# Weight block rows 528 bytes apart, and two tiles of one projection in 256-column products

## The chip, the cores and the metric

The kernel runs on one core of a Trainium2 chip. The metric is the device time of one execution in microseconds (us), smaller is better; the program has one launch. A core has five engines that work side by side and wait for each other through semaphores: TensorE multiplies matrices (its matrix work is "PE" in the profile, the loading of the stationary operand is "PEld"), VectorE is "DVE", ScalarE is "ACT", GpSimd is "POOL", and SyncE, "SP", mostly issues DMA transfers between HBM and the on-chip memory SBUF. TensorE reads both operands from SBUF and writes its sums into PSUM.

One matmul instruction of this kernel has a *stationary* operand (128 partitions by 128 columns, loaded first) and a *moving* operand (128 partitions by up to 512 columns, streamed past it). Both are rows of 4-byte numbers in each of the 128 partitions; where such a row begins within a partition is its address.

## The reference

The reference is one encoder block for 1024 tokens of width 1024 in float32, with d_ff = 2816:

```python
h = layer_norm(x, ln_in_g, ln_in_b)
proj = h @ w_in[l]                                  # 1024 x 11776, one combined projection
att = dilated_attention(aq, ak, av, slopes)         # 512 wide
rec = hgrn2(hq, hf_fwd, hf_bwd, hi, hg, ...)        # 1024 wide, chunkwise recurrence
merged = sigmoid(ga) * (att @ w_att_up[l]) + sigmoid(gh) * (rec @ w_hgrn_up[l])
h = layer_norm(ALPHA * h + merged @ w_o[l], ...)
gate, up = split(h @ w_ffn_in[l], 2, axis=-1)
h = layer_norm(ALPHA * h + (silu(gate) * up) @ w_ffn_out[l], ...)
```

## The kernel before

**Products.** Every large matrix product is done with numbers split in two: `hi` is the value rounded to the type float32r, `lo` is the rest. `mm3` (lines 270 to 274) issues three matmuls for one block: hi with hi (line 272), the stationary hi with the moving lo (line 273), the stationary lo with the moving hi (line 274). Such a matmul of 128x128 by 128x512 is called a *product* here; there are 7596 of them. `split` (line 211 on) makes the pair: ScalarE casts (line 214), then GpSimd or VectorE subtracts (line 224).

**Granules.** `granules` (line 253) hands out a pair of tiles `w_hi` and `w_lo` of 128 x 4 x 128 numbers from the pool `wp`: four weight blocks side by side, 2048 bytes a partition, with four buffers of each, so eight tiles. A block is 512 bytes of a partition. `weights`, `prep` in `stream`, `product` in `wino_project`, `next_weights` and the row tiles of the W_o stage all take their stationary blocks from there. In `ffn_out` the inner function `weights` (line 1889 on) takes the same tiles flat, as one 512-column moving operand, and the stationary blocks come from the pool `ws`.

**Where tiles lie.** Pools are stacked from two sides of SBUF: `wp` is the first from the right, and all other pools of the right side lie below it; constants are the first from the left. Two pads, `CST_PAD` of 32 bytes and `SMT_PAD` of 704 bytes, shift the left side. In the compiled program the stationary and the moving operand of each of the 7596 products begin 480 bytes past a multiple of 512. The difference of the two addresses modulo 512 bytes is called the *place* here; before the change it is 0 in every product.

**Stages.** Phase 0 and 1 (up to about 1162 us): the input layer norm and the combined projection, done by `stream` with a seven-product form of block matrix multiplication for each 2 x 2 group of blocks; between its groups the attention and recurrence units issue small float32 matmuls and transposes. Phase 2: `att @ W_a` (192 products, 1168.3 to 1211.8 us), in eight tiles `d`, each two halves of 512 tokens by four blocks by three products through `project_many` (line 279); then `rec @ W_r` and the product with W_o. Phase 3: `ffn_in` with the seven-product form, 84 products a step (7 by 4 blocks by 3), and `ffn_out`.

**Order.** A planner with a cost model orders the instructions of each engine when the program is built. Some orders are written by hand (`behind`, `ordered`, `queued`), and evacuations of PSUM run at high priority. Weights are split three products ahead (`prep(i + 3)`).

Of the kernel before, what the change touches and what calls it, by code (L numbers as in the profile page):

```python
# [11 lines left out]
F32R = mybir.dt.float32r  # L12
# [10 lines left out]
HALF = 512  # L23
# [56 lines left out]
class Block:  # L80
# [169 lines left out]
    def queued(self, dst, src):  # L250
        self.ordered("loads", self.nc.sync.dma_start(dst, src))

    def granules(self, pool=None, bufs=4):

        p = pool or self.wp
        return [p.tile([128, 4, 128], F32R, name=n, tag=n, bufs=bufs) for n in ("w_hi", "w_lo")]

    def weights(self, w, r0, nk, c0, pool=None, bufs=2, tag="wraw"):

# [7 lines left out]
            out += [(hi[:, k, :], lo[:, k, :]) for k in range(4)]  # L267
        return out

    def mm3(self, ps, whi, wlo, xhi, xlo, first, last, **kw):  # L270
        nc = self.nc
        nc.tensor.matmul(ps, whi, xhi, start=first, stop=False, **kw)  # L272
        nc.tensor.matmul(ps, whi, xlo, start=False, stop=False, **kw)  # L273
        self.product = nc.tensor.matmul(ps, wlo, xhi, start=False, stop=last, **kw).ins.name  # L274
# [1114 lines left out]
    def phase2(self):  # L1389
        nc = self.nc  # L1390
        with ExitStack() as es:
# [14 lines left out]
            def mrow(k, h):  # L1406
                return m1[:, k, :] if h else m0[k // 2][:, k % 2, :]
            sp = self.sp

            def tgate(i):  # L1410
                t = sp.tile([128, T], F32, name="tg", tag="gate", bufs=2)
                nc.sync.dma_start(t, self.tg_d[i])
                return t

            def up(d):
                return self.weights(self.wa, 0, 4, 128 * d, bufs=1, tag=f"wraw{d % 2}")

            wa = [up(0), up(1)]
            for d in range(8):
                t = tgate(d)  # L1420

                def evac(h, ps, d=d, t=t):
                    s = slice(HALF * h, HALF * (h + 1))
                    nc.vector.scalar_tensor_tensor(mrow(d, h), t[:, s], 1.0, ps, op0=OP.add, op1=OP.mult)

                self.load_split(sp, self.rec_d[d], self.rh[:, d, :], self.rl[:, d, :])
                self.project_many([(self.wa, 4, 128 * d, evac, wa.pop(0))], self.ah, self.al)
                if d < 6:
                    wa.append(up(d + 2))
            wo = [[mp.tile([128, KT, HALF], F32R, name=f"wo0{n}") for n in ("hi", "lo")]]  # L1430
# [17 lines left out]
            for d in range(8):  # L1448
                t = tgate(8 + d)
# [8 lines left out]
                c = d // 2 + 4 * (d % 2)  # L1458
# [11 lines left out]
            for z in (rows, self.recp, self.stp):  # L1470
# [4 lines left out]
                       for n in ("t1", "b11", "b21", "t2")}  # L1475
            yp = es.enter_context(self.pool("yp"))
            w11 = [(yp if k < 3 else self.ws).tile([128, HALF], F32, name="w11", tag=f"w11{k}" if k < 3 else "wsum",
                                                   bufs=1 if k < 3 else 3) for k in range(4)]
# [330 lines left out]
    def ffn_out(self):  # L1809
# [4 lines left out]
        nc, NP = self.nc, NF // 2  # L1814
        with ExitStack() as es:
# [25 lines left out]
            loaded, raws, ready, last, t2s = 0, {}, {}, {}, {}  # L1841
# [32 lines left out]
                return hi, lo  # L1874

            def weights(src):
                hi, lo = (z.rearrange("p k c -> p (k c)") for z in self.granules())
                self.split(hi, lo, src, eng_lo="dve", key="sums")
                return hi, lo

# [12 lines left out]
            def prep(i):  # L1893
                nonlocal loaded
                if i >= len(seq):
                    return
                p, f = seq[i]
                a = acts(p, f)
                while i and loaded < min(len(loads), 4 + 3 * i // 2):
                    load(*loads[loaded])  # L1900
                    loaded += 1
                src = t2s[f] if p == 6 else W[{1: "11", 2: "21", 5: "11", 7: "12", 3: "22"}[p], f]
                ready[i] = a, weights(src)
                for z in todo.get(i, ()):
                    extra(*z)
# [44 lines left out]
            for i, (p, f) in enumerate(seq):  # L1950
# [3 lines left out]
                if p in (1, 6) and 4 <= f < 8:  # L1954
                    t = f if p == 6 else f - 4
                    self.queued(Y[t], self.ahs_d[t])
                if p == 5 and f < 2:
                    t, v = (g2, b2)[f], self.ln["2"][f]
                    self.queued(t, bass.AP(tensor=v.tensor, offset=v.offset, ap=[[0, 128], [1, D]]))
                for g in range(4):  # L1960
                    if f == 0 and p == 2:
                        banks[g][1] = self.ps_sd()
                    c = slice(128 * g, 128 * (g + 1))
# [25 lines left out]
            for c, (g, f0) in enumerate(chunks):  # L1989
# [4 lines left out]
                for k in range(min(4, NP - f0)):  # L1994
                    z = slice(128 * k, 128 * (k + 1))
                    self.mm3(banks[g][0], ahi[:, z], alo[:, z], *last[f0 + k], False, f0 + k == NP - 1,
                             skip_group_check=True)
# [45 lines left out]
```

## Time and profile before

| what | value |
|---|---|
| time, three runs | 2034.79, 2037.7 and 2040.7 us; median 2037.7 us |
| profiled execution | span of 2034.2 us from the first to the last instruction; no other time of it is given |
| granted TensorE clock, mean | 0.998 of full speed |
| products of 512 columns | 7596, about 0.227 us from one start to the next |
| matmuls in all, as recorded | 11002 |
| HBM traffic | 200.77 MB read, 94.11 MB written |

The span leaves out what lies around the program's first and last instruction; beside the median of the runs it is 3.5 us shorter. In the group rows a matmul's own duration includes its way through the array and overlaps the next one, so the pace is read from starts: a product that shows 389 ns begins about 227 ns after the one before it. Float32 matmuls (the small ones) are recorded as two passes.

### The profile page before, as it was taken

The numbers are of one execution on the slowest core, as the hardware profiler recorded it, in microseconds if no ns is written. First come the engines' busy times: TensorE is split into PE (matmuls) and PEld (weight loads), VectorE is DVE, ScalarE is ACT, GpSimd is POOL, SyncE is SP. The second block draws the span as 40 slices with busy tenths as digits, with TensorE's granted clock in tenths as the row PEclk, the third lists the DMA queues.
The fourth block names the chain that finished last, engine by engine and source line by source line (L and its number), as shares of the span: only waits on it lengthen the run. The fifth ranks groups of instructions, "written<-read, shape, count | busy, mean of one in ns | idle before, by whom it ended". The sixth has DMA issues, their size and how long they took to land. (4 is left out here: it accounts for less than half of the span.)

```text
span 2034.2 us, 31011 instructions
## 1 busy us (share of the span) xinstructions
PE 2005.5 (99%) x11002; PEld 1666.0 (82%) x11002; DVE 1310.3 (64%) x2065; ACT 961.4 (47%) x1980; POOL 1026.6 (50%) x890
## 2 busy tenths in 40 slices
PE   7999999999999999999999999999999999999998
PEld 5788888788888888888888888888788888888886
DVE  7777545884458843778444226557776776767788
ACT  6654455554655535665465433244433333344541
POOL 6656644676446663466545662244765665630000
PEclk9999999999999999999999999999999999999999
DMA  5443533445333453343534477444434443447533
GB/s 160 153 137 120 174 118 109 132 135 171 119 123 125 135 170 104 125 141 125 170 99 149 132 258 234 143 144 141 139 135 140 135 140 130 129 168 288 165 98 126
DMA packets 274430, 296.93 MB, mean 146 GB/s; under 512 B 14113, under 2 KB 207458, under 8 KB 274274
## 3 DMA queue, kind: packets, MB, share of 16 engines
q1 hardware_dynamic: 267968, 273.73, 42.2%
q10 hardware_dynamic: 6306, 21.20, 2.7%
q8 instruction: 87, 1.43, 0.3%
q14 instruction: 69, 0.57, 0.1%
HBM read 200.77 MB, written 94.11 MB: 145 GB/s over the span
## 5 line engine op out<-in xcount | busy, mean ns | idle before, releaser
L224 POOL TENSOR_TENSOR w_lo<-wa,w_hi 128x512 fp32r<-128x512 f32 x272 | 364.4, 1349 | 273.5 <-ACT w_hi L214 235.0
L214 ACT CAST w_hi<-wa 128x512 fp32r<-128x512 f32 x272 | 168.7, 621 | 252.8 <-PE pj L273 151.5
L224 POOL TENSOR_TENSOR w_lo<-wsum,w_hi 128x512 fp32r<-128x512 f32 x88 | 127.9, 1464 | 111.1 <-PE sd L274 60.7
L224 POOL TENSOR_TENSOR w_lo<-f_raw,w_hi 128x512 fp32r<-128x512 f32 x66 | 101.2, 1540 | 51.5 <-ACT w_hi L214 50.3
L210 POOL TENSOR_TENSOR mv<-mv,mhalf 128x1 f32<-128x1 f32 x16 | 12.7, 792 | 221.7 <-DVE mv L209 218.6
L214 ACT CAST w_hi<-wsum 128x512 fp32r<-128x512 f32 x88 | 54.6, 621 | 116.7 <-PE sd L273 108.8
L214 ACT CAST gwsum<-a_raw 128x512 fp32r<-128x512 f32 (+1 forms) x78 | 48.2, 618 | 112.5 <-PE pj L273 54.1
L272 PE MATMUL pj<-xt1hi,w_hi 128*128 128x512 f32 x252 | 99.8, 396 | 0.0
L274 PE MATMUL pj<-xt1hi,w_lo 128*128 128x512 f32 x252 | 98.7, 392 | 0.0
L273 PE MATMUL pj<-xt1lo,w_hi 128*128 128x512 f32 x252 | 98.4, 391 | 0.0
L224 POOL TENSOR_TENSOR w_lo<-ws,w_hi 128x512 fp32r<-128x512 f32 x46 | 64.5, 1406 | 55.1 <-ACT w_hi L214 54.8
L583 DVE TENSOR_TENSOR evh<-wkeep,pj 128x512 f32<-128x512 f32 x45 | 30.8, 685 | 95.3 <-PE pj L274 55.5
L698 POOL TENSOR_TENSOR wa<-wa,wa 128x512 f32<-128x512 f32 x46 | 67.5, 1469 | 48.9 <-DVE wa L697 45.6
L572 DVE TENSOR_TENSOR evh<-wkeep,pj 128x512 f32<-128x512 f32 x66 | 58.0, 882 | 39.7 <-PE pj L274 29.4
L726 ACT COPY wkeep<-pj 128x512 f32<-128x512 f32 x136 | 79.4, 585 | 2.0 <-DVE evh L572 2.0
L274 PE MATMUL pj<-xt2hi,w_lo 128*128 128x512 f32 x192 | 75.8, 395 | 2.5 <-POOL w_lo L224 2.5
L273 PE MATMUL pj<-xt2lo,w_hi 128*128 128x512 f32 x192 | 75.5, 393 | 1.3 <-DVE xt2lo L404 1.3
L272 PE MATMUL pj<-xt2hi,w_hi 128*128 128x512 f32 x192 | 76.0, 396 | 0.7 <-ACT w_hi L214 0.7
L224 DVE TENSOR_TENSOR gwkeep<-a_raw,gwsum 128x512 fp32r<-128x512 f32 (+1 forms) x78 | 53.1, 680 | 36.5 <-ACT gwsum L214 33.7
L272 PE MATMUL pj<-xb11hi,w_hi 128*128 128x512 f32 x192 | 76.0, 398 | 0.4 <-DVE evh L583 0.4
L272 PE MATMUL pj<-xt4hi,w_hi 128*128 128x512 f32 x192 | 76.3, 397 | 0.0
L273 PE MATMUL pj<-xb11lo,w_hi 128*128 128x512 f32 x192 | 75.5, 394 | 0.0
(449 smaller groups left out, 6584.1 us busy)
## 6 DMA issues: line engine op xcount, KB each, us to landing
wa<-in_w_in_dram SPq DMA_DIRECT2D x184, 256.0 KB, 3.3
f_raw<-in_w_ffn_in_dram SPq DMA_DIRECT2D x44, 512.0 KB, 4.2
a_raw<-gd SPq DMA_DIRECT2D x30, 512.0 KB, 3.7
gd<-fc SPq DMA_DIRECT2D x44, 256.0 KB, 2.0
gd<-fs SPq DMA_DIRECT2D x33, 256.0 KB, 2.6
tg<-evh SPq DMA_DIRECT2D x32, 256.0 KB, 2.4
tg<-tg SPq DMA_DIRECT2D x16, 512.0 KB, 5.7
y<-ahs SPq DMA_DIRECT2D x16, 512.0 KB, 6.9
```

The lines of the kernel that those rows point to most:

```text
L210: nc.gpsimd.tensor_tensor(mv[:, 2:3], mv[:, 2:3], self.mhalf[:, 0:1], OP.pow)
L214: ins = nc.scalar.copy(hi, src) if eng_hi == "act" else nc.vector.tensor_copy(hi, src)
L224: ins = e.tensor_sub(lo, src, hi.bitcast(F32))
L272: nc.tensor.matmul(ps, whi, xhi, start=first, stop=False, **kw)
L273: nc.tensor.matmul(ps, whi, xlo, start=False, stop=False, **kw)
L274: self.product = nc.tensor.matmul(ps, wlo, xhi, start=False, stop=last, **kw).ins.name
L572: self.left(nc.vector.tensor_tensor(o, self.order_src(add, g, kind), s, OP.add))
L583: self.left(nc.vector.tensor_add(t, add, ps))
L698: nc.gpsimd.tensor_sub(a["a21"], a["a22"], a["a11"])
L726: nc.scalar.copy(t, ps)
```

## The change

`granules` allocates tiles with rows of 132 numbers and hands out the first 128 of each. The four blocks of a tile begin 528 bytes apart rather than 512, and a tile takes 2112 bytes of a partition rather than 2048. The eight tiles therefore begin 64 bytes further apart modulo 512, and the four blocks in each another 16 bytes: 32 places, each 16-byte step once. The pool grows by 512 bytes in all, so that the other tiles of the right side move by exactly 512 bytes. Where `ffn_out` wants a flat operand, it gets the first 512 numbers of the tile, so its moving operand is in one piece and its place is one of eight.

The second edit sets a flag for the tiles d = 3 and 4 of `att @ W_a`. With it `mm3` issues each product as two of 256 columns, with the same stationary block, into the two halves of the same PSUM bank.

```diff
-    def granules(self, pool=None, bufs=4):
+    def granules(self, pool=None, bufs=4, flat=False):
         p = pool or self.wp
-        return [p.tile([128, 4, 128], F32R, name=n, tag=n, bufs=bufs) for n in ("w_hi", "w_lo")]
+        t = [p.tile([128, 4, 132], F32R, name=n, tag=n, bufs=bufs) for n in ("w_hi", "w_lo")]
+        if flat:
+            return [z.rearrange("p k c -> p (k c)")[:, 0:HALF] for z in t]
+        return [z[:, :, 0:128] for z in t]
...
+    narrow = False
+
     def mm3(self, ps, whi, wlo, xhi, xlo, first, last, **kw):
         nc = self.nc
+        if self.narrow:
+            kw["skip_group_check"] = True
+            for n, (w, x) in enumerate(((whi, xhi), (whi, xlo), (wlo, xhi))):
+                for h in range(2):
+                    z = slice(256 * h, 256 * h + 256)
+                    self.product = nc.tensor.matmul(ps[:, z], w, x[:, z], start=first and n == 0 and h == 0,
+                                                    stop=last and n == 2 and h == 1, **kw).ins.name
+            return
...
+                self.narrow = d in (3, 4)
                 self.project_many([(self.wa, 4, 128 * d, evac, wa.pop(0))], self.ah, self.al)
+                self.narrow = False
...
             def weights(src):
-                hi, lo = (z.rearrange("p k c -> p (k c)") for z in self.granules())
+                hi, lo = self.granules(flat=True)
```

## The prediction

> **What bounds the kernel now.** I read the page's busy times first, then who TensorE waits for, then the chain that ended last, and last the pace of single products.
>
> ```profile
> span 2034.2 us, 31011 instructions
> ...
> PE 2005.5 (99%) x11002; PEld 1666.0 (82%) x11002; DVE 1310.3 (64%) x2065; ACT 961.4 (47%) x1980; POOL 1026.6 (50%) x890
> ```
>
> ```profile
> PE pj L274 <- POOL w_lo L224: 4.0, 5, 1.6
> ...
> PE pj L272 <- ACT w_hi L214: 0.7, 1, 0.7
> ```
>
> TensorE is busy in 99% of the span, and the longest it waited in total for a weight half is 4.0 us. So the time is the number of matmuls times their pace, and a change of the pace goes into the end one to one. In the chain of waits the same product comes back once per step of `ffn_in`, which has 84 products:
>
> ```profile
> 1481.04 0.45 PE sd L274 x2
> ...
> 1804.72 0.45 PE sd L274 x2
> ```
>
> Between the first and the last of these rows lie 17 steps: (1804.72 - 1481.04) / (17 x 84) = 0.22667 us a product. It is the same pace in other stages, to the nanosecond, with other tiles as moving operand; in these rows (from the views by source line; minimum, median and maximum duration in ns) a record of 389 ns belongs to a start-to-start step of 227:
>
> ```profile
> L272 PE MATMUL pj<-att_hi,w_hi x64: 389/389/389, 1168.3 to 1211.1; 128*128 128x512 f32 x64
> ...
> L273 PE MATMUL pj<-rec_lo,w_hi x128: 389/389/389, 1212.0 to 1298.4; 128*128 128x512 f32 x128
> ```
>
> Phase 1 has the same median, but a spread:
>
> ```profile
> L273 PE MATMUL pj<-xb21lo,w_hi x176: 387/389/499, 116.1 to 1409.0; 128*128 128x512 f32 x176
> ```
>
> The timeline shows where that comes from (start, duration, both in us). Small matmuls break the row of products; when the products begin again it takes about ten of them to come back to the old pace:
>
> ```profile
> 264.80 0.83 PE L873 MATMUL sd<-k,q 64*64 64x128 f32 x24
> 265.57 0.50 PE L272 MATMUL pj<-xb21hi,w_hi 128*128 128x512 f32 x1
> 265.91 0.40 PE L273 MATMUL pj<-xb21lo,w_hi 128*128 128x512 f32 x1
> 266.15 0.40 PE L274 MATMUL pj<-xb21hi,w_lo 128*128 128x512 f32 x1
> ...
> 268.00 0.39 PE L273 MATMUL pj<-xb21lo,w_hi 128*128 128x512 f32 x1
> 268.24 0.39 PE L274 MATMUL pj<-xb21hi,w_lo 128*128 128x512 f32 x1
> 268.46 0.39 PE L272 MATMUL pj<-xb21hi,w_hi 128*128 128x512 f32 x1
> 268.69 0.39 PE L273 MATMUL pj<-xb21lo,w_hi 128*128 128x512 f32 x1
> ```
>
> From 265.91 to 268.24 there are ten products (the one at 268.24 not counted): 2.33 / 10 = 0.233 us each, with steps up to 0.24 (265.91 to 266.15). After that the step is 0.227 again. No engine is waited for in these ten. So the pace of a product isn't one number: there is a settled pace of 226.7 ns and an unsettled one of about 233 ns, and what differs is only how the load and the stream of the products before have met in time. All of that is at place 0; a 512-column product at another place doesn't occur in this trace.
>
> **The change part by part.** *Places.* 7464 products get a stationary or moving tile from a granule with a moved address (7596 less the 132 of the last product of `ffn_out`, whose two operands come from other pools). Work is neither added nor removed; the stream is still 512 columns and the load still 128. The cost is what the place does to the pace, and this has to be bounded. From below: the shortest record in the row of xb21lo is 387 ns, 2 ns under the settled 389. From above: the longest step of the unsettled row, 0.24 us, 13.3 ns over 226.7. Zero lies inside. I choose from the row that is nearest to the new situation. Load and stream run at the same time from the same memory; if how they meet in time is worth 6 ns, as the ten unsettled products show, then where they read is likely to be worth something too, and in the new kernel the place changes between nearly all neighbours (the four blocks of a tile are 16 bytes apart in place, `w_hi` and `w_lo` come from tiles that differ by multiples of 64), so that there is no steady relation to settle into. That gives the unsettled pace, 233.0 - 226.7 = 6.3 ns, to the products that don't settle. Some neighbours will have places that keep the settled pace; nothing tells how many, and I take one in four: 0.75 x 6.3 = 4.7 ns on average, 7464 x 4.7 = 35 us. Phase 1 pays some of this already after its breaks: the group row
>
> ```profile
> L273 PE MATMUL pj<-xt1lo,w_hi 128*128 128x512 f32 x252 | 98.4, 391 | 0.0
> ```
>
> has a mean of 391 against the median of 389, which over the 3864 products of phase 1 is 2 x 3864 = 7.7 us, and part of that is the 499 of the first product after a break, which stays. I take off 3 us. Left: +32 us.
>
> *256 columns.* Tiles 3 and 4 have 2 x 2 x 4 x 3 = 48 products, which become 96 matmuls with as many loads. No 256-column matmul of this type is in the trace. Small passes with a load of the same size bound it:
>
> ```profile
> 904.92:909.75 4.83, 4.83 (x44) 4.83 (x43) 1.00 0.31 102
> ...
> 308.88:309.80 0.92, 0.92 (x8) 0.92 (x8) 1.00 0.80 285
> ```
>
> The first row (windows, of line 1265 alone) has 44 passes of 128 columns in 4.83 us, 110 ns each; the second (line 965) has eight passes of 32 columns in 0.92 us, 115 ns. A quarter of the columns saves nothing, so both go at the pace of the 128-column load, and a load a matmul can be had every 110 to 115 ns. Half of a product is 113 ns. From below a pair takes 2 x 110 = 220 ns, 48 x -6.7 = -0.3 us; from above, if nothing were gained by the shorter stream, a pair takes 2 x 226.7 and the edit costs 48 x 226.7 = 10.9 us. The rows of the loads speak against the upper end, and I take 2 x 115 = 230: +0.2 us. The evacuation and its wait are the same, since the last of the 96 still carries the stop. By the Trainium skill (TensorE: Matmul & The Clock Gate, Back-to-back issue gap) an isolated warm matmul takes N/2.4 + 2.5 ns, which would be 215.8 for 512 columns and 109.2 for 256, so that the pair would cost 48 x 2.6 = 0.1 us; the trace has 226.7 rather than 215.8 for the first, so the formula is 11 ns short for this type.
>
> *Splits.* ScalarE, GpSimd and VectorE now write `w_hi` and `w_lo` in four pieces of 128 numbers. Such an output is there already, where the splits of h write a 128-column slice of a wider tile:
>
> ```profile
> L214 ACT CAST w_hi<-wa 128x512 fp32r<-128x512 f32 x272 | 168.7, 621 | 252.8 <-PE pj L273 151.5 <-POOL w_lo L224 30.7 <-issue 24.2
> ...
> L214 ACT CAST xb11hi<-tsv 128x512 fp32r<-128x512 f32 x4 | 2.6, 638 | 0.0
> ...
> L224 POOL TENSOR_TENSOR w_lo<-wa,w_hi 128x512 fp32r<-128x512 f32 x272 | 364.4, 1349 | 273.5 <-ACT w_hi L214 235.0 <-PE sd L1013 6.6 <-DMA wa<-in_w_in_dram 6.2
> ...
> L224 POOL TENSOR_TENSOR xb11lo<-tsv,xb11hi 128x512 fp32r<-128x512 f32 x3 | 4.2, 1390 | 5.2 <-ACT xb11hi L214 5.2
> L224 POOL TENSOR_TENSOR xb21lo<-tsv,xb21hi 128x512 fp32r<-128x512 f32 x3 | 3.9, 1289 | 0.0
> ```
>
> Between no difference and 17 ns on ScalarE, between -60 and +41 on GpSimd. I take zero. The cover is the three products by which `prep` runs ahead, 3 x 12 x 226.7 ns = 8 us for a split of 2 us; without it each of about 500 splits would add up to 60 ns, 30 us, but ScalarE is 47% and GpSimd 50% busy and TensorE waits for them 4.7 us in the rows above. No DMA, queue or wait is added or moved; the pool's 512 bytes shift its neighbours by a whole 512, so their places stay. If TensorE slows down, all other engines gain slack, and nothing else is late.
>
> **Sum.** 2034.2 (span) + 32 + 0.2 = 2066.4 us; the median of the runs is 3.5 us above this span: 2070 us.
>
> **The rivals.** *The place does nothing* (28%). The load doesn't notice it in the small passes:
>
> ```profile
> L965 PEld LDWEIGHTS sd<-NL,perm 128*128 128x128 f32 x32 | 3.9, 191 | 0.7 <-issue 0.7
> ...
> L1213 PEld LDWEIGHTS sd<-hv,hkT 128*128 128x128 f32 x224 | 27.4, 191 | 1.3
> ```
>
> In the compiled program line 965 is at place 128 and line 1213 at place 0, and both loads take 191 ns. And 389/389/389 holds while DMA and three engines use the memory. Against it: these small passes go at the load's pace, so a stream held up by some ns would not show in them. Time: 2034.2 + 3.5 + 0.2 = 2038 us. The Trainium skill has this rule too (SBUF — State Buffer, Who interferes with whom): TensorE has two independent read ports, one for each operand, and waits on nobody. The att rows agree as far as other engines go; for the two operands against each other no row here can show it, since all are at place 0.
>
> *Place 0 is a bad place* (10%): load and stream begin on the same spot of memory and hold each other up, and spreading takes this away. Price from rows: 387 instead of 389, 7464 x -2 = -15 us, 2034.2 - 15 + 3.7 = 2023 us; it decides from a gain of 0.8 ns a product on (6 us over 7464). For it: the unsettled row has steps under the settled one. Against it: more are above.
>
> *Every product at the top of the unsettled range* (part of the slower case, 6%): 13.3 ns x 7464 - 3 = +96 us, 2134 us. For it: the first step after a break is 0.24 and each change of place may be such a break. Against it: the next steps are already shorter.
>
> **How the numbers follow.** Slower 62%: its own range goes from 2048 (a quarter of the unsettled excess) to 2105 (halfway from 6.3 to 13.3 ns, 9 ns x 7464 = 67 us). A measurement of this kernel tells about 0.3%, 6 us, from no change. The place without effect is the "same" case, 28%; the gain is the 10%. The range 2030 to 2105 takes in the slower case without its top, the case without effect, and the smallest gains.
>
> **What would show it.** Right: records of `att`, `rec` and `ffn_in` products with a spread of some 387 to 402 instead of 389/389/389, a mean of 393 to 395, and a step of `ffn_in` of 19.4 to 19.6 us rather than 19.04; 96 records of half width 110 to 120 ns apart; TensorE's waits unchanged. Wrong: 389/389/389 everywhere (no effect), records under 387 (the gain), or new waits of TensorE for `w_lo`, which would mean that the splits or the planner's order have become the matter.

## The result, and the profile after

The changed kernel takes 2066.8 us (median of four runs, 2066.59 to 2071.59), the kernel before beside it 2037.8 us. The ratio is 1.0152, with a 95% interval of 1.0137 to 1.0167: it is slower by about 29 us. The profiled execution has a span of 2064.8 us, 30.6 us more than before, at the same granted clock of 0.998.

The page of the changed kernel, and then TensorE's waits for weight halves (us in total, times, longest):

```profile
span 2064.8 us, 31105 instructions
...
PE 2039.2 (99%) x11050; PEld 1670.5 (81%) x11050; DVE 1310.2 (63%) x2065; ACT 962.0 (47%) x1980; POOL 1024.5 (50%) x890
```

```profile
PE pj L287 <- POOL w_lo L224: 2.9, 4, 1.5
...
PE pj L285 <- ACT w_hi L214: 0.6, 1, 0.6
```

TensorE has 33.7 us more of busy time (2039.2 against 2005.5), while ScalarE, GpSimd and VectorE have what they had. It waits for weights no longer than before. So nothing new holds TensorE up from outside; its own products take longer. The rows by source line (minimum, median and maximum in ns, first and last start) and the chain of waits show it:

```profile
L286 PE MATMUL pj<-rec_lo,w_hi x128: 387/393/404, 1226.2 to 1314.4; 128*128 128x512 f32 x128
L286 PE MATMUL pj<-xb21lo,w_hi x176: 387/394/496, 117.2 to 1427.1; 128*128 128x512 f32 x176
```

```profile
1507.47 0.24 PE pj L286
1515.87 0.24 PE sd L286
1519.38 0.46 PE sd L287 x2
...
1830.91 0.47 PE sd L287 x2
```

The pace is read from such a row in this way: in `rec @ W_r` the same line comes back every third product, so between the first and the last start of 128 records lie 381 products, (1314.4 - 1226.2) / 381 = 231.5 ns each. The row of before gives (1298.4 - 1212.0) / 381 = 226.8. In `ffn_in` 16 steps lie between the last two rows of the chain: (1830.91 - 1519.38) / (16 x 84) = 231.8 ns against 226.7. The uniform 389/389/389 has become a spread, and the timeline of `rec @ W_r` (start and duration) shows that the steps no longer repeat evenly:

```profile
1239.68 0.39 PE L287 MATMUL pj<-rec_hi,w_lo 128*128 128x512 f32 x1
1239.90 0.39 PE L285 MATMUL pj<-rec_hi,w_hi 128*128 128x512 f32 x1
1240.13 0.39 PE L286 MATMUL pj<-rec_lo,w_hi 128*128 128x512 f32 x1
1240.37 0.39 PE L287 MATMUL pj<-rec_hi,w_lo 128*128 128x512 f32 x1
```

Steps of 0.22, 0.23 and 0.24 us stand side by side, with no break before them.

Where the 30.6 us lie: over all starts of records, a step under 300 ns between two products was on average 227.9 ns in phase 1 before and 232.05 after, 4.2 ns x 3515 steps = 14.6 us. Behind phase 1 it was 226.8 and is 231.8 (the half-width records left out), 5.1 ns x 3726 steps = 18.9 us. That is 33.5 us together. The other 3 us go the other way, in the steps over 300 ns and the breaks between rows of products; this rest wasn't divided further.

The 256-column records show up in the rows by source line as

```profile
L282 PE MATMUL pj<-att_hi,w_hi x32: 274/280/297, 1198.0 to 1208.7; 128*128 128x256 f32 x32
L282 PE MATMUL pj<-att_lo,w_hi x32: 277/280/287, 1198.2 to 1208.9; 128*128 128x256 f32 x32
```

Their mean step is 118.07 ns (113 to 124, and one of 133), so 48 pairs cost 48 x (2 x 118.07 - 226.67) = 0.45 us against products at place 0. The splits in four pieces cost what they cost before. These are the groups of the page, with the mean of one in ns behind the busy time:

```profile
L214 ACT CAST w_hi<-wa 128x512 fp32r<-128x512 f32 x272 | 168.6, 620 | 263.8 <-PE pj L286 158.7 <-POOL w_lo L224 39.9 <-issue 20.1
...
L224 POOL TENSOR_TENSOR w_lo<-wa,w_hi 128x512 fp32r<-128x512 f32 x272 | 366.1, 1354 | 283.9 <-ACT w_hi L214 245.8 <-PE sd L1226 7.0 <-PE sd L1026 6.6
```

620 and 1354 ns, against 621 and 1349.

### The profile page after: what moved, and what is told of

It is laid out like the page before. It is cut to its first block, busy times and chain, and to the rows that moved or that the text cites. A ratio compares the mean times of both kernels' runs of the same rounds, so it can differ in the third digit from the quotient of the medians.

```text
span 2064.8 us, 31105 instructions
## 1 busy us (share of the span) xinstructions
PE 2039.2 (99%) x11050; PEld 1670.5 (81%) x11050; DVE 1310.2 (63%) x2065; ACT 962.0 (47%) x1980; POOL 1024.5 (50%) x890
## 5 line engine op out<-in xcount | busy, mean ns | idle before, releaser
L224 POOL TENSOR_TENSOR w_lo<-wa,w_hi 128x512 fp32r<-128x512 f32 x272 | 366.1, 1354 | 283.9 <-ACT w_hi L214 245.8
```

The source lines that it names most:

```text
L224: ins = e.tensor_sub(lo, src, hi.bitcast(F32))
```

## The experiments

In what follows a place is the address of the stationary operand less that of the moving one, modulo 256 bytes where nothing else is said; why 256 is shown in the second group. In the changed kernel `w_hi` and `w_lo` of a pair lie four tiles apart, 4 x 2112 = 8448 bytes, which is 0 modulo 256. So the three products of a block share a place, and in `att`, `rec` and W_o it changes after every third product.

### The two edits apart

`rows_only` has the rows of 528 bytes without the 256-column products, `narrow_only` these without the rows:

```diff
# rows_only, against the changed kernel
-                self.narrow = d in (3, 4)
+                self.narrow = False
# narrow_only, against the changed kernel
-        t = [p.tile([128, 4, 132], F32R, name=n, tag=n, bufs=bufs) for n in ("w_hi", "w_lo")]
+        t = [p.tile([128, 4, 128], F32R, name=n, tag=n, bufs=bufs) for n in ("w_hi", "w_lo")]
```

> The 528-byte rows alone; tiles 3 and 4 of att @ W_a keep 512 columns. My theory (the place of the operands sets the pace): all of the change but half a microsecond stays, span 2064.3, about 1.5% over before. Rival (the 256-column tiles or the planner's order bring the loss): back towards 2034.

> The 256-column tiles alone; rows of 512 bytes, so place 0 everywhere. My theory: a 256-column step of 115 to 118 ns, 48 x (2 x 118 - 226.7) = +0.4 us, span 2034.7, the same as before within what can be measured. Rival (the narrow tiles or another order made by the planner cost something elsewhere): 2 us or more.

`rows_only` took 2065.8 us, ratio 1.0136 (1.012 to 1.0151), and the product of `rec @ W_r` 231.5 ns: the whole slowdown is in the rows. `narrow_only` took 2036.7 us, ratio 1.0 (0.9989 to 1.001). At place 0 the half-width products are as regular as the full ones:

```profile
L282 PE MATMUL pj<-att_lo,w_hi x32: 283/283/283, 1183.4 to 1194.3; 128*128 128x256 f32 x32
L282 PE MATMUL pj<-att_hi,w_lo x32: 283/283/283, 1183.7 to 1194.6; 128*128 128x256 f32 x32
```

94 of the 96 steps are 120 ns long. 512 columns take 226.67 and 256 take 120.0. A straight line through these two widths has 106.7 ns for 256 columns, 0.417 ns a column, and 13.3 ns for each product besides; a third width wasn't tried. The edit alone costs 48 x 13.3 = 0.6 us, too little to be told.

### One place for a whole stage

My theory was that a pace above 226.7 comes from *change*: neighbours at different places never settle. The rival: each place has its own price, changed or not. With rows of 512 bytes and a pad ahead of the moving tiles, all products of a stage get one and the same place, other than 0:

```diff
# surveyA (modulo 512: phase 1 at 256, att and ffn_in at 448, rec at 320)
+        self.pad(self.ws, 256)
...
+                    self.pad(ap, 64)
...
+            self.pad(self.wraw, 128)
...
+            self.pad(self.rawp, 32)
...
+            self.pad(rp, 128)
# surveyB (phase 1 at 32, att and ffn_in at 128, rec at 64): the same pads with 32, 384, 32, 64, 64
```

> Rows of 512 bytes again; pads shift whole pools, so that each stage has one constant place: phase 1 256 bytes, att, the second half of W_o and ffn_in 448, rec 320, the first half of W_o 160, ffn_out 384. Theory 1 (the change of place between neighbours keeps products from settling): every stage settles at 226.7 ns, span about 2034. Theory 2 (the place itself sets the pace): stages settle at paces of their own, away from 226.7, 229 to 236 ns, span 2050 to 2090. Theory 3 (block starts that are no multiple of 32 bytes, or the row stride of 528): all stages at 226.7.

> As the run before with other constant places: phase 1 32 bytes, att, the second half of W_o and ffn_in 128, rec 64, the first half of W_o 96, ffn_out 480. Theory 1: 226.7 ns in all stages, span about 2034. Theory 2: paces away from 226.7, other ones than in the run before. Theory 3: 226.7 in all stages.

`surveyA` took 2049.6 us (1.0056; 1.0041 to 1.0071) and `surveyB` 2075.7 us (1.0184; 1.0167 to 1.0201), more than the change itself, though no place changes within a stage. The third theory falls with it: here the rows are 512 bytes and the block starts are multiples of 32. Rows by source line, first of `surveyA`, then of `surveyB`:

```profile
L273 PE MATMUL pj<-rec_lo,w_hi x128: 388/396/398, 1211.6 to 1300.5; 128*128 128x512 f32 x128
L273 PE MATMUL pj<-att_lo,w_hi x64: 388/388/397, 1167.7 to 1211.0; 128*128 128x512 f32 x64
```

```profile
L273 PE MATMUL pj<-rec_lo,w_hi x128: 388/396/398, 1231.3 to 1320.2; 128*128 128x512 f32 x128
L273 PE MATMUL pj<-att_lo,w_hi x64: 392/395/398, 1186.5 to 1230.6; 128*128 128x512 f32 x64
```

In both kernels `rec` takes 88.9 us / 381 = 233.3 ns a product, at place 320 in the one and 64 in the other. That two places 256 bytes apart agree comes back at 192 and 448 below, and phase 1 at 256 settles on 226.7 as at 0: the price repeats every 256 bytes. `att` takes 43.3 / 189 = 229 ns at 448 and 44.1 / 189 = 233 at 128.

So a constant place does settle, but on a short cycle. The groups of `surveyA` within the `att` stage show the cycle of three, since it runs in step with the three lines of `mm3` (busy us, mean ns of one):

```profile
L274 PE MATMUL pj<-att_hi,w_lo 128*128 128x512 f32 x64 | 25.1, 392 | 0.0
L272 PE MATMUL pj<-att_hi,w_hi 128*128 128x512 f32 x64 | 25.0, 394 | 0.0
L273 PE MATMUL pj<-att_lo,w_hi 128*128 128x512 f32 x64 | 24.9, 388 | 0.0
```

The steps there are 226, 229 and 232 ns, again and again. At 64 they are 236 and 231 in turn. At 128 the cycle isn't the same everywhere: in `att` of `surveyB` 229 and 238 come in turn (233.3 on average), while long rows of `ffn_in` run through seven steps, 232, 228, 230, 233, 241, 232 and 231 (232.4).

### The map, filled in

`surveyC` and `surveyD` lay the hi and the lo half of the moving operands into one tile that begins some numbers past its start, which gives places down to 4 bytes:

```diff
+    def joint(self, pool, name, n, off, tag=None):
+        t = pool.tile([128, 2 * n + 64], F32R, name=name, tag=tag or name, bufs=1)
+        return [t[:, off + i * n:off + i * n + n] for i in range(2)]
...
-            self.rh, self.rl = (rp.tile([128, KT, T], F32R, name=n) for n in ("rec_hi", "rec_lo"))
+            self.rh, self.rl = (z.rearrange("p (k c) -> p k c", k=KT) for z in self.joint(rp, "rec_", KT * T, 52))
```

> Constant places again, now odd multiples of 16 bytes: att 16, rec 48, the first half of W_o 80, the second 112, ffn_in 144 (some tiles 400, the same modulo 256); phase 1 at 192, ffn_out at 0. If the period is 256 bytes, phase 1 settles at 228.9 ns as at 448. If place 0 is the best, no stage is under 226.7 and most lie at 229 to 235; a stage under 226.7 would be the way to a faster kernel.

> The rest of the places: att 176, rec 208, the first half of W_o 240, the second 8, ffn_in 4 (some tiles 260); phase 1 at 160, ffn_out at 0. Phase 1 should settle at about 233.3 ns as the first half of W_o did at 160. If only whole 16-byte steps count, places 4 and 8 give 226.7 as place 0 does; if single numbers count, they give something of their own.

They took 2053.8 us (1.0074; 1.0049 to 1.01) and 2065.0 us (1.0138; 1.0122 to 1.0154). Rows by source line of `surveyC` (rec at 48, att at 16), and of the chain of waits of `surveyD` (`ffn_in` at 4 and 260):

```profile
L273 PE MATMUL pj<-rec__11903,w_hi x128: 395/397/398, 1218.4 to 1307.9; 128*128 128x512 f32 x128
...
L273 PE MATMUL pj<-att__11416,w_hi x64: 392/398/403, 1173.0 to 1217.7; 128*128 128x512 f32 x64
```

```profile
1507.17 0.45 PE sd L274 x2
...
1835.61 0.46 PE sd L274 x2
```

att at 16: 44.7 / 189 = 236.5 ns; rec at 48: 89.5 / 381 = 234.9. At 4 bytes: (1835.61 - 1507.17) / (17 x 84) = 230.0. All four surveys together, mean step in ns from the starts of the records of each stage (undisturbed steps, so that a value can differ by some tenths from that of the rounded rows):

| place | 0 | 4 | 8 | 16 | 32 | 48 | 64 | 80 | 96 | 112 |
|---|---|---|---|---|---|---|---|---|---|---|
| ns | 226.7 | 230 | 233 | 236.7 | 233.4 | 234.7 | 233.3 | 233.2 | 234.0 | 233.3 |

| place | 128 | 144 | 160 | 176 | 192 | 208 | 224 | 240 |
|---|---|---|---|---|---|---|---|---|
| ns | 232.4 to 233.3 | 231 | 233.3 | 231.1 | 228.9 | 233.3 | 233.3 | 231.7 |

No place is under 226.7, and of those tried only 0 reaches it. The mean over the sixteen multiples of 16 is 232.6, or 232.2 when each counts as often as it occurs in the changed kernel; that kernel has 231.95 over all its undisturbed steps.

The sum agrees, but its parts don't. The records of the changed kernel can be sorted by the place that each product has in the compiled program. Behind phase 1, `ffn_out` left out, some 160 to 185 steps fall on each place:

| place | 0 | 16 | 128 | 176 | least and most of the sixteen |
|---|---|---|---|---|---|
| held for a whole stage, ns | 226.7 | 236.7 | 232.4 to 233.3 | 231.1 | 226.7 and 236.7 |
| in the changed kernel, ns | 230.7 | 232.0 | 234.3 | 229.6 | 229.6 and 234.3 |

`rows_only` gives 231.0, 231.9, 234.4 and 229.5 at these four. So a product in the changed kernel doesn't go at the pace that its place has when it is held: the best place loses 4 ns there, and the worst gains nearly 5.

### What counts: the difference, and the change

`alt256` puts the lo moving tiles 256 bytes from the hi ones, so that places 0 and 256 (modulo 512) come in turn. `both64` moves stationary and moving tiles by 64 bytes alike.

```diff
# alt256, in phase 1; in phase 3 the same way
+        lo = [self.xp.tile([128, 4, HALF], F32R, name=f"x{n}lo", tag=f"x{n}lo", bufs=1) for n in names]
+        self.pad(self.xp, 256)
+        hi = [self.xp.tile([128, 4, HALF], F32R, name=f"x{n}hi", tag=f"x{n}hi", bufs=1) for n in names]
# both64
+        if self.low:
+            self.pad(self.wp, self.low)
...
+                    self.pad(ap, 448)
...
+            self.pad(fob, 448)
```

> Rows of 512 bytes. In four of the seven products of phase 1 and in three of ffn_in (those with t1, b11, b21, t2; of t4 all) the moving lo tiles lie 256 bytes away from the hi tiles, so that the place goes 0, 256, 0 from product to product; both places settled at 226.7 ns when held. If the relation modulo 256 bytes alone decides and a change between neighbours is free: 226.7 ns in long rows, span 2034. If a change of place costs by itself (the step of my prediction): about 232 in four of seven products, span about 2050.

> Both operands of all products lie 64 bytes lower modulo 512 (416 rather than 480), so the place stays 0. If only the difference of the two addresses counts: 226.7 ns, span 2034. If the addresses themselves count (64 bytes was a slow place in the survey): about 233 ns, span about 2075.

`alt256`: 2036.3 us, 1.0002 (0.9992 to 1.0011). `both64`: 2037.1 us, 1.0003 (0.9993 to 1.0013). Of the chain of waits of `alt256`, and by source line of `both64`:

```profile
1481.42 0.45 PE sd L274 x2
...
1690.87 0.45 PE sd L274 x2
```

```profile
L278 PE MATMUL pj<-rec_lo,w_hi x128: 389/389/389, 1215.7 to 1302.1; 128*128 128x512 f32 x128
```

(1690.87 - 1481.42) / (11 x 84) = 226.7 ns. In the groups concerned two of three neighbours differ by 256 bytes (29% of all neighbours in the kernel), and it costs nothing. But as the price repeats every 256 bytes, 0 and 256 are one place: this shows that the pace goes modulo 256, and not that a change between unlike places is free. In `both64` the address itself made no difference, only the distance of the two, as far as one shift of 64 bytes at place 0 can tell.

### Unequal places in turn

If each product paid the price of its own place, kernels with places in turn would show the average. A load can also meet the stream of the product before it, so that the place of the *next* block against the present stream might be what counts. `cross64` tells these two apart: with lo tiles 64 bytes below the hi ones, for weights as well as moving tiles, the own places of att and rec are 0, 64 and 192, 229.6 ns on average by the map, while the place to the next load is always 0.

```diff
+        lo = p.tile([128, 4, 128], F32R, name="w_lo", tag="w_lo", bufs=bufs)
+        if self.gap:
+            self.pad(self.wp, self.gap)
+            self.gap = 0
+        return [p.tile([128, 4, 128], F32R, name="w_hi", tag="w_hi", bufs=bufs), lo]
```

> Rows of 512 bytes; w_lo and the moving lo tiles of att, rec and phase 1 lie 64 bytes below their hi tiles. In att and rec a product's own stationary and moving operand are then at places 0, 64 and 448 in turn, but each stationary block is at place 0 to the moving operand of the product before, during whose stream it is loaded. If the load meets the stream of the product before: att and rec at 226.7 ns in all steps, and phase 1, whose next places are all 64, at about 233.3 in long rows. If a product's own two operands meet: att and rec at (226.7 + 233.3 + 228.9) / 3 = 229.6, phase 1 (own places 64, 128, 0) at about 230.9.

It took 2072.3 us, 1.0167 (1.0151 to 1.0183). By source line:

```profile
L278 PE MATMUL pj<-rec_lo,w_hi x128: 395/395/395, 1229.4 to 1318.3; 128*128 128x512 f32 x128
```

88.9 / 381 = 233.3 ns, in a cycle of 236, 232 and 232: neither 226.7 (the next load) nor 229.6 (the own places). Phase 1 took 232.9, between the 233.3 and the 230.9 that the two rules gave. Both simple rules fall by `rec`, and places in turn cost 3.7 ns more there than the average of their own prices.

`tiles64` and `tiles128` leave the blocks of a tile 512 bytes apart and change the place only from tile to tile, by 64 or by 128 bytes:

```diff
-        return [p.tile([128, 4, 128], F32R, name=n, tag=n, bufs=bufs) for n in ("w_hi", "w_lo")]
+        t = [p.tile([128, 528], F32R, name=n, tag=n, bufs=bufs) for n in ("w_hi", "w_lo")]    # tiles64; 544 in tiles128
+        return [z[:, 0:512].rearrange("p (k c) -> p k c", k=4) for z in t]
```

> Rows of 512 bytes again, but the eight tiles of the weight pool begin 64 bytes apart modulo 512: places 0, 64, 128, 192 modulo 256, which change from product to product. If the price of a product is that of its place as held constant in the surveys (0, 6.7, 6.0 and 2.2 ns over 226.7) and a change is free: 1872 x 6.7 + 1872 x 6.0 + 1828 x 2.2 = 28 us less 3 that phase 1 pays already, span about 2059. If a change between neighbours costs too: 2066 or more.

> As the run before with tiles 128 bytes apart: two places modulo 256, 0 and 128, the same for w_hi and w_lo of a pair, so it changes only every twelve products. By the prices of the surveys: about 3700 products at +6.1 ns less some 3 us, span about 2054. If a new place also costs a row of unsettled products in those that go back to 0 (ten steps of 233 of each twelve): nearly all are slow, span about 2070.

The text for `tiles64` is wrong in one point: `w_hi` and `w_lo` of a pair lie 256 bytes apart modulo 512 there, so the place changes only from tile to tile, not from product to product.

`tiles64`: 2064.9 us, 1.0132 (1.0116 to 1.0149), span 2061.3. `tiles128`: 2060.0 us, 1.0113 (1.0094 to 1.0133), span 2058.1. By source line, one row of each:

```profile
L274 PE MATMUL pj<-rec_lo,w_hi x128: 389/394/404, 1224.0 to 1311.8; 128*128 128x512 f32 x128
```

```profile
L274 PE MATMUL pj<-rec_lo,w_hi x128: 387/390/404, 1222.3 to 1310.4; 128*128 128x512 f32 x128
```

The prices of the constant places had given spans of 2059 and 2054; measured are 2 and 4 us more, which by itself is within the 5 us by which executions of one kernel differ here. The single steps tell more. Sorted by the own place, the products of `tiles128` take 232.85 ns at 128, as on the map, but 229.2 ns at 0 instead of 226.7. In `tiles64` it is 229.4 at 0, 233.0 at 64, 232.6 at 128 and 230.4 at 192. So products at the good place lose some of it when they stand among others. In `rec` of `tiles128` this can be followed: twelve products at 128, twelve at 0, and so on. The first of a twelve at 0 begins at 1227.56 us:

```profile
1227.56 0.40 PE L273 MATMUL pj<-rec_hi,w_hi 128*128 128x512 f32 x1
1227.80 0.39 PE L274 MATMUL pj<-rec_lo,w_hi 128*128 128x512 f32 x1
1228.02 0.39 PE L275 MATMUL pj<-rec_hi,w_lo 128*128 128x512 f32 x1
1228.26 0.40 PE L273 MATMUL pj<-rec_hi,w_hi 128*128 128x512 f32 x1
1228.49 0.39 PE L274 MATMUL pj<-rec_lo,w_hi 128*128 128x512 f32 x1
1228.72 0.40 PE L275 MATMUL pj<-rec_hi,w_lo 128*128 128x512 f32 x1
1228.95 0.39 PE L273 MATMUL pj<-rec_hi,w_hi 128*128 128x512 f32 x1
1229.18 0.39 PE L274 MATMUL pj<-rec_lo,w_hi 128*128 128x512 f32 x1
1229.41 0.39 PE L275 MATMUL pj<-rec_hi,w_lo 128*128 128x512 f32 x1
```

The middle of the row of the kernel before, between the lines that the prediction shows of the products after a break:

```profile
266.62 0.40 PE L273 MATMUL pj<-xb21lo,w_hi 128*128 128x512 f32 x1
266.85 0.39 PE L274 MATMUL pj<-xb21hi,w_lo 128*128 128x512 f32 x1
267.08 0.39 PE L272 MATMUL pj<-xb21hi,w_hi 128*128 128x512 f32 x1
267.31 0.40 PE L273 MATMUL pj<-xb21lo,w_hi 128*128 128x512 f32 x1
267.55 0.39 PE L274 MATMUL pj<-xb21hi,w_lo 128*128 128x512 f32 x1
267.77 0.40 PE L272 MATMUL pj<-xb21hi,w_hi 128*128 128x512 f32 x1
```

The views round to 10 ns; from the starts in the traces, in ns, the steps are:

| row | steps |
|---|---|
| `before`, place 0 throughout, from 266.62 us | 236, 224, 231, 236, 228, 232, 231, 227, 227, 226 |
| `tiles128`, place 0 after twelve products at 128, from 1227.56 us | 236, 224, 231, 236, 228, 233, 231, 226, 227, 227 |

It is the same row. After a change back to place 0 the products settle as they do after a break, here in seven steps; on average over `rec` the first seven steps at 0 take 231.0 ns and the next four 226.7 (the text above had named ten steps of 233). In `rec` of `tiles64` three steps are enough (227.5, 229.2, 229.0). In the changed kernel a place holds for about three products only, so there is little room to settle. That is the part of my theory of change that holds.

### Half the load

Last, whether the price lies in the load of the stationary operand. In `halfload` att is at place 64 and rec at 0, and the second and the third product of each three load only 64 of the 128 columns. If the price is a share of the load's time, it should halve at 64.

```diff
+            nc.tensor.matmul(ps, whi, xhi, start=first, stop=last, **kw)
+            nc.tensor.matmul(ps[0:64], whi[:, 0:64], xlo, start=False, stop=False, **kw)
+            self.product = nc.tensor.matmul(ps[0:64], wlo[:, 0:64], xhi, start=False, stop=last, **kw).ins.name
```

> In att @ W_a (held at place 64) and rec @ W_r (at place 256, which goes as 0) the second and third product of each block use only the first 64 columns of the stationary block, so that the lo terms of the upper 64 output rows are left out; the stream stays 512 columns. 512 columns alone take 213.3 ns by the 256-column run ((226.7 - 120.0) x 2). If the 13.3 ns above that are paid by the stream for the load that runs beside it: steps with a half load pay half, 220.0 ns in rec, the full ones 226.7; in att about 223 and 233. If it is a fixed price of each matmul: 226.7 ns in all steps of rec, 233.3 on average in att. The rest of the kernel runs at place 64 in ffn_in (233.3), so its time is no comparison.

The kernel ran once, in 2053.9 us, so only paces within it are read. The groups of the loads within `rec @ W_r` (busy us, mean ns), then the products by source line:

```profile
L276 PEld LDWEIGHTS pj<-rec_hi,w_hi 128*128 128x128 f32 x128 | 24.0, 188 | 12.4
L278 PEld LDWEIGHTS pj<-rec_hi,w_lo 128*64 128x64 f32 x128 | 17.2, 134 | 12.0
```

```profile
L277 PE MATMUL pj<-rec_lo,w_hi x128: 389/397/398, 1216.5 to 1303.9; 128*64 128x512 f32 x128
L277 PE MATMUL pj<-att_lo,w_hi x64: 392/397/398, 1172.1 to 1215.8; 128*64 128x512 f32 x64
```

The shorter load takes 54 ns less, and the products don't gain by it: 43.7 / 189 = 231.2 ns at 64, and 87.4 / 381 = 229.4 ns at place 256, which goes as 0; this is *slower* than the 226.7 with whole loads. A price in proportion to the load and a fixed price both fall. But here loads of 128 and of 64 columns come in turn, so that the change between them may itself cost something; that wasn't separated. How load and stream hold each other up stays open; what could separate it further (the load's own length in more sizes, or loads without a stream) wasn't tried.

No version tried was faster than the kernel before; the three that come out even (`narrow_only`, `alt256`, `both64`) have place 0 or 256 throughout.

## Why the prediction was right, and where its reason was wrong

**The bound holds.** TensorE is the bound before and after (99%), and a pace that was 4 to 5 ns longer went into the end: 33.5 us of longer steps, 30.6 us of span.

**The size came out partly by luck.** The forecast was +32.2 us on the span and 2070 us; measured are +30.6 and 2066.8. Its step was 0.75 x 6.3 = 4.7 ns a product, less 3 us, and both factors were off. Measured over the undisturbed steps are 231.95 - 226.7 = 5.3 ns, about 39 us over 7464 products. From this comes off what phase 1 paid already, 1.2 ns x 3515 = 4 us (the prediction took 3), and the 3 us in the long steps. So a too small excess and a too small deduction nearly cancelled. "One in four" keeps the settled pace is wrong as well: sorted by place, none of the sixteen does, the quickest takes 229.6 ns.

**What of "change" is right.** The prediction said that products whose place changes between neighbours find no steady relation and go at the unsettled pace. `tiles128` bears this out: a change from 128 back to 0 puts the products through the very row of steps that a break does. In the changed kernel products at place 0 take 230.7 ns and those at 16 take 232.0, where held places give 226.7 and 236.7. `alt256` is no evidence against it, since 0 and 256 are one place.

**What was wrong in it.** The prediction knew one settled pace, 226.7 ns, and one unsettled pace of 233, and gave the whole loss to change. The surveys show that a loss needs no change: places other than 0, held for a whole stage, settle on cycles with a mean of 229 to 237 ns, and `surveyB` lost more than the change did. So the 6.3 ns, taken from products that were on their way back to place 0, say nothing of the other fifteen places; that they are near 5.3 is chance. It is chance too, as far as these runs show, that the held prices add up to nearly the right sum: 232.6 - 226.7 = 5.9 ns over 7464 products is 44 us, 5.5 ns and 41 us when each place counts as often as it occurs. What sets the single step of a product among unlike places stays open.

**The time around the span.** The prediction added 3.5 us to the span. Each execution for which both are given takes about 1.8 us more than its span (2066.59 against 2064.8), so the rest of the 3.5 was most likely the distance of the profiled execution of before from the median. That is about half of the 3 us between 2070 and 2066.8.

**A slip in the range.** Halfway from 6.3 to 13.3 ns is 9.8 ns, 73 us, not 9 ns and 67 us; the upper end would have been 2111 rather than 2105. The result doesn't depend on it.

**256 columns.** 115 ns for a half were taken, 118.07 measured, and 120.0 at place 0; +0.45 instead of +0.2 us, inside the bounds. The step went by the pace of the small passes, 110 to 115 ns, and that was not the nearest row: a line through both widths at place 0 has 0.417 ns a column and 13.3 ns on top. By the Trainium skill (TensorE: Matmul & The Clock Gate, Back-to-back issue gap) the slope is the same, N/2.4, and what is added for an isolated matmul is 2.5 ns; here it is 13.3 by that line, so the measurement decides.

**Splits, queues and waits.** At nothing, as put: 620 and 1354 ns a split against 621 and 1349, and 3.5 us of waiting for weights against 4.7.

**The signs named ahead.** The records of `rec` show 387/393/404, with means of 393 and 394 by line (387 to 402 and a mean of 393 to 395 were named), a step of `ffn_in` is (1830.91 - 1519.38) / 16 = 19.47 us (19.4 to 19.6), the half-width records lie 118 ns apart on average (110 to 120 were named), and no new wait has come.

**The rivals.** "The place does nothing" falls by `rows_only` and the surveys. The row that spoke for it, small passes at place 128 with the same load of 191 ns, was no evidence: the loads' own records didn't show the price in the slow kernels either (187/188/192 in `rec` of the changed kernel, in the row below), it shows between the starts. "Place 0 is bad" falls: no other place is better. "All at the top" falls too: single steps reach 13 ns more, a mean nowhere, and the worst place has 10. The 0.24 us that the prediction calls the first step after a break is the second; the first, from 265.57 to 265.91, took 0.34.

```profile
L286 PEld LDWEIGHTS pj<-rec_lo,w_hi x128: 187/188/192, 1226.0 to 1314.2; 128*128 128x128 f32 x128
```

## What to carry to other kernels

In a kernel like this one, where products with a load each run back to back, the address of the stationary operand relative to the moving one deserves attention: for these 512-column products equal addresses modulo 256 bytes were the best of the places tried, and any other place, held, cost 1 to 4% of the pace. A mixture of places isn't priced by the average of its parts, so measure the mixture. The loss shows in no wait and no load record, only in the spread of records that should be identical (389/389/389 against 387/393/404), in the distance of their starts and in TensorE's total. Before a tile's row is padded for another reason, count what it does to the addresses of all blocks behind it.

## What the hardware showed that was not expected

- The price of a held place has a period of 256 bytes (226.7 at 0 and 256, 233.3 at 64 and 320, 228.9 at 192 and 448) and goes by the difference of the two addresses; both moved by 64 bytes cost nothing.
- It isn't symmetric, 233.3 ns at 64 and 228.9 at 192, and no smooth function: the worst place is 16 (236.7), and 4 bytes already cost 3.3 ns.
- A constant place gives a short repeating cycle of steps (236, 231; 226, 229, 232; 229, 238), not one longer step, and at 128 two different cycles were seen (233.3 and 232.4 ns).
- After a break and after a change of place from 128 to 0, the products come back to 226.7 ns through the same row of steps (236, 224, 231, 236, 228, 232, 231).
- Half-width products are on average quicker at mixed places (118.1 ns) than at place 0 (120.0), the other way round than full ones.
- Loading half of the stationary columns in two of three products shortens these loads by 54 ns and makes the products at place 256 longer, 229.4 instead of 226.7 ns.
